# Both gates' projections moved out of the input projection into a stage of seven half-size products

## The chip, the cores and the metric

The kernel runs on one core of one Trainium2 chip. The metric is the device time of one execution in microseconds. Matrix products run on TensorE (PE in the profile), the other arithmetic on VectorE (DVE), ScalarE (ACT) and GpSimd (POOL). SyncE (SP) issues nearly all transfers.

## What is computed

A decoder layer with two parallel groups of heads over 1024 tokens of width 2048. One projection gives the inputs of both groups and their gates z_a and z_g:

```python
h = jnp.einsum('bsd,de->bse', x, w_in[l])
q_a, k_a, v_a, z_a, q_g, k_g, v_g, z_g, gk_lr = jnp.split(h, pts, axis=-1)
...
y_a = _swa_sink_attention(q_a', k_a', v_a', attn_sinks[l]) * jax.nn.silu(z_a)
...
y_g = (o_g.astype(x.dtype) * jax.nn.silu(z_g.reshape(B, S, GLA_HEADS, GLA_DV))).reshape(B, S, GLA_WIDTH)
y = jnp.einsum('bse,ed->bsd', jnp.concatenate([y_a, y_g], axis=-1), w_out[l])
x = _layer_norm(DN_ALPHA * x + y, ln_g[l], ln_b[l])
```

(The primes stand for the rotary positions.) Attention has 16 query heads of 64, 2 key heads, a window of 128 and a sink for each head. The second group is gated linear attention (GLA): 4 heads with keys of 128 and values of 256, a data-dependent decay, and an RMS norm on each head's output. z_a and z_g have 1024 columns each: together 2048 of the 5392 columns of w_in.

## The kernel before

Every fp32 product is three matmuls. `split` (L108) turns a tile into a rounded part, cast on ACT, and the rest, a subtraction on DVE; high x high, high x low and low x high are summed in PSUM.

The **input stage** runs the tokens in two halves H of 512. `half_jobs` (L491) makes a list of jobs from ORDER (L42), and each job projects x to 128 output features (K, V: the attention keys and values; a: a query tile of two heads; z: the attention gate of a tile; q, k: GLA; g, h: the two halves of a GLA head's gate) or, for v, to 256. `main_f` (L165) does a job in 48 matmuls of 128x512 into one of the three banks of the pool mm; `main_v` does a v job in 192 of 128x256. Behind each job its `evac` takes the bank over, and its `later` functions are put off by so many jobs (`run_later`, L648): attention of a query tile comes one job behind its projection, the stages of a GLA head (`gla_near`, `gla_far`, two `gla_pairs`) nought to three jobs behind v. A gate job's evac makes SiLU with tanh (`silu2`), multiplies it with the mixer's output (`attention_out`, `gla_out`) and stores the gated result to DRAM (`store_y`, buffer yd).

The mixers have one buffer of nearly everything. One attention head goes: ps (scores on PE), s (ACT copies, DVE puts in the masked part), nm (row maximum, DVE), four exponentials (ACT), s times the reciprocal sum (POOL, L278), pt (four transposes on PE), pm (DVE masks the transposed tile), po (the product with the values on PE). A GLA head begins with gk, the decays' product (`decays`), goes through seven levels of operands w and products pa, the transposes pk and the state products pg and pkv, and ends in the transposes po of `gla_out`. All of ps, pt, gk, pa, pk, pkv and the GLA po share the three banks of the pool sd; so has two.

`weight_sums` (L627), one for every second job, makes with four GpSimd subtractions the sums of blocks of w_out that the output stage needs, 32 in all, and stores them to DRAM (td). They and the projection weights come through the four raw buffers.

The **output stage** does y x w_out with seven products of half size in place of eight (Strassen in Winograd's form). `seq` (L818) has their order. Each runs over two column halves fp, eight k and four tiles t, 3 matmuls each (`product`, L739), into eight banks: the three of mm and five of op, which take the place of so and sd. `y_part` loads and adds blocks of y (POOL, L721), `w_part` loads eight weight tiles (pool wsp) for a half, and `collect` adds each product to its outputs. The layer norm runs behind the last ones.

The engines' orders are set when the program is built: a planner orders the instructions by its own estimates and by priority, which is the place in the program, raised by `high_priority` for loads and splits. On the chip each engine keeps that order and waits where something isn't ready.

Of the kernel before, what the change touches and what calls it, by code (L numbers as in the profile page):

```python
# [31 lines left out]
E_QA, E_KA, E_VA, E_ZA, E_QG, E_KG, E_ZG = 0, 8, 9, 10, 18, 22, 26  # L32
# [9 lines left out]
ORDER = [  # L42
    "K V q0 k0 v0 a0 z0 a1 z1 g0 h0 a2 z2 q1 k1 v1 a3 z3 g1 h1 a4 z4 q2 k2 v2 a5 z5 g2 h2 a6 z6 q3 k3 v3 a7 z7 g3 h3",
    "K V q0 k0 v0 a0 z0 a1 z1 g0 h0 a2 z2 q1 k1 v1 a3 z3 g1 h1 a4 z4 q2 k2 v2 a5 z5 g2 h2 a6 z6 q3 k3 v3 a7 z7 g3 h3",
]
# [30 lines left out]
def build(ctx: ExitStack, tc, xT, xr, w_e, w_v, w_gk, w_up, b_gk, cos_d, sin_d, cst_d, sinks, wn_d, w_out, g_d, b_d, out):  # L76
# [83 lines left out]
    td = [dr_p.tile([P, 16, 4, 256], F32, name=f"td{f}") for f in range(2)]  # L160
    ys_d = dr_p.tile([P, 8 * T], F32, name="ysum")
# [28 lines left out]

    def silu2(acc, pool, tag, bufs):

        t = pool.tile([P, T], F32, name=tag, tag=tag, bufs=bufs)
        A.activation(t, acc, AF.Tanh, scale=0.5)
        V.scalar_tensor_tensor(t, t, 1.0, acc, ALU.add, ALU.mult)
        return t
# [101 lines left out]
    def store_y(y, H, f):  # L298
        SP.dma_start(yd[H][f // 4][:, (f % 4) * T:(f % 4 + 1) * T], y)
# [166 lines left out]
    def gla_out(hd, gen, sz, H):  # L466
        for pr, on in gen:
            pt = sd.tile([P, 2, 2, P], F32, name="po", tag="sd")
            for u in range(2):
                for i in range(2):  # L470
                    PE.transpose(pt[:, u, i], on[:, i, u * P:u * P + P], ident)
            for u in range(2):
                c = slice(2 * pr * P, 2 * pr * P + 2 * P)
                z = sz[u][:, c].rearrange("p (i q) -> p i q", i=2)
# [16 lines left out]
    def half_jobs(H):  # L491
        c = ctxs[H]

        def qa(t):
# [5 lines left out]
            e_job(H, E_QA + t, evac, (None, later))  # L500

        def za(t):
            e_job(H, E_ZA + t, lambda acc: attention_out(t, c.pop(("po", t)), acc, H))
# [14 lines left out]
        def v_job(hd):  # L518
# [17 lines left out]
            jobs.append(Job([w_v[hd][:, :2048], w_v[hd][:, 2048:]], H, "v", evac, (near, far, pair, pair)))  # L536

        def zg(hd, u):
            def evac(acc):
                c["sz", hd, u] = silu2(acc, gp, f"szg{u}", 1)  # L540

            def later():
                gla_out(hd, c["on", hd], [c["sz", hd, 0], c["sz", hd, 1]], H)
            e_job(H, E_ZG + 2 * hd + u, evac, (None, later) if u else ())
# [7 lines left out]
        make = {"K": ka, "V": va, "q": q_job, "k": k_job, "v": v_job, "g": lambda hd: zg(hd, 0), "h": lambda hd: zg(hd, 1), "a": qa, "z": za}  # L552
        for j in ORDER[H].split():
            make[j[0]](*map(int, j[1:]))
# [72 lines left out]
    def weight_sums(n):  # L627

        f, k, u = n // 16, n % 16 // 2, n % 2
# [3 lines left out]
        for t, (eg, q) in ((b11, (f, 0)), (b12, (2 + f, 0)), (b21, (f, 2)), (b22, (2 + f, 2))):  # L633
            SP.dma_start(t, w_out[eg, q + k // 4][:, c])
# [4 lines left out]
        SP.dma_start(td[f][:, n % 16], r)  # L639
# [14 lines left out]
    i = 0  # L654
    while i < n:
# [43 lines left out]
    G.memset(eps, LN_EPS)  # L699

    def y_raw(h, g, k, tag):

        r = x_p.tile([P, T], F32, name="yr", tag=tag)
        with tc.high_priority(2000):
            SP.dma_start(r, yd[h][2 * g + k // 4][:, (k % 4) * T:(k % 4 + 1) * T])
        return r

    def y_part(i, k):

        at = {1: "00", 2: "01", 3: "01", 4: "11", 5: "10", 6: "10", 7: "00"}[i]  # L710
        a = y_raw(int(at[0]), int(at[1]), k, "xh")
        kept = ys_d[:, k * T:k * T + T]
        if i == 3:
            b = x_p.tile([P, T], F32, name="yr", tag="xl")
            with tc.high_priority(2000):
                SP.dma_start(b, kept)
            G.tensor_tensor(a, a, b, ALU.subtract)
        more = {5: ((1, 1, 1),), 6: ((1, 1, 1), (0, 0, -1)), 7: ((1, 0, -1),)}
        for n, (h, g, sign) in enumerate(more.get(i, ())):
            b = y_raw(h, g, k, "xl" if n % 2 == 0 else "xh")  # L720
# [5 lines left out]
    def w_part(i, fp, q, pool, tag):  # L726

        r = raw_p.tile([P, 2, 512], F32, name="raw", tag="raw")
        with tc.high_priority(2000):
            if i in (1, 2, 3):  # L730
                eg, w = {1: (fp, 0), 2: (fp, 2), 3: (2 + fp, 2)}[i]
                src = w_out[eg, w + q // 2][:, (q % 2) * 1024:(q % 2) * 1024 + 1024]
                SP.dma_start(r, src.rearrange("p (u c) -> p u c", u=2))
            else:
                j = {5: 0, 7: 1, 4: 2, 6: 3}[i]
                SP.dma_start(r.rearrange("p u (h c) -> p (u h) c", h=2), td[fp][:, 4 * q:4 * q + 4, j])
        return [split(r[:, u], pool, tag) for u in range(2)]

    def product(acc, y, w, t, k, first, last):  # L739
        (yh, yl), (wh, wl) = y, w  # L740
        c = slice(t * P, t * P + P)
        PE.matmul(acc, yh[:, c], wh, start=(first and k == 0), stop=False, skip_group_check=True)  # L742
# [169 lines left out]
```

## Time and profile before

| | us |
|---|---|
| median of 3 runs | 1437.87 (1437.31 to 1441.54) |
| the profiled execution | 1435.88 |
| its span, first to last instruction | 1433.7 |
| TensorE busy | 1414.9 (99%) |
| VectorE busy | 856.7 (60%) |
| ScalarE busy | 600.3 (42%) |
| GpSimd busy | 290.3 (20%) |

The input stage takes the first 1111 us, the output stage the rest. Matmul durations overlap in the trace, since PE is pipelined: what a matmul costs is read from the distance of the starts. A row of the timeline names the engine, the line, and out<-in by the program's names.

### The profile page before, as it was taken

What the parts mean: (1) busy time and instruction counts of PE and PEld (TensorE: products, weight loads), DVE (VectorE), ACT (ScalarE), POOL (GpSimd) and SP (SyncE); (2) the same over time, 40 slices, a digit from 0 to 9 for tenths busy, and PEclk for the clock granted to TensorE, in tenths of its full rate; (3) what the DMA queues carried; (4) which work ended last, traced back from release to release, by engine and by line L of the source; (5) the groups of instructions that cost most, each with busy time, mean ns of one, the idle gap of its engine ahead of it and who ended that gap; (6) DMA issues with size and microseconds to landing.
All of it is one profiled execution on the core that took longest, in us unless ns stands there. A gap on an engine that the chain in (4) does not pass through costs nothing.

```text
span 1433.7 us, 23435 instructions
## 1 busy us (share of the span) xinstructions
PE 1414.9 (99%) x8992; PEld 1181.0 (82%) x8992; DVE 856.7 (60%) x1481; ACT 600.3 (42%) x1279; POOL 290.3 (20%) x325
## 2 busy tenths in 40 slices
PE   8999999999999999999999999999999999999996
PEld 5888889888888976898888888988898888888885
DVE  5565556555655566565655555564566645466798
ACT  5544435435443445344435443443545324433320
POOL 0032212221311122213212221131101412122000
PEclk9999999999999999999999999999999999999998
DMA  8243344443434435543443334433325797665552
GB/s 318 86 148 128 111 147 131 135 133 107 144 131 134 133 127 175 168 157 113 159 133 123 115 131 136 138 112 118 104 95 163 239 362 230 216 218 189 172 208 117
DMA packets 99231, 222.36 MB, mean 155 GB/s; under 512 B 10800, under 2 KB 43568, under 8 KB 97968
## 3 DMA queue, kind: packets, MB, share of 16 engines
q1 hardware_dynamic: 97968, 218.78, 46.1%
q10 hardware_dynamic: 1152, 2.10, 0.4%
q8 instruction: 70, 1.15, 0.3%
q14 instruction: 41, 0.34, 0.1%
HBM read 180.47 MB, written 35.65 MB: 151 GB/s over the span
## 4 chain that ended last, share of the span: by engine, by line
PE 98%; DVE 1%; DMA 1%; ACT 0%; POOL 0%; SPq 0%; issue 0%; DVEq 0%; POOLq 0%
PE acc L172 18%; PE acc L174 18%; PE acc L173 17%; PE acco L742 7%; PE acco L743 7%; PE acco L744 7%; PE accv L186 4%; PE accv L188 4%; PE accv L187 4%; PE po L291 2%; PE pa L360 1%; PE ps L259 1%; PE ps L260 1%; PE pt L281 1%; PE lracc L310 1%; PE pg L405 1%
## 5 line engine op out<-in xcount | busy, mean ns | idle before, releaser
L113 DVE TENSOR_TENSOR wl<-raw,wh 128x512 fp32r<-128x512 f32 x440 | 331.6, 759 | 280.7 <-ACT wh L112 258.1
L112 ACT CAST wh<-raw 128x512 fp32r<-128x512 f32 x440 | 269.8, 620 | 416.9 <-PE acc L173 283.5
L172 PE MATMUL acc<-xh,wh 128*128 128x512 f32 x1088 | 429.4, 396 | 6.5 <-ACT wh L112 6.5
L174 PE MATMUL acc<-xh,wl 128*128 128x512 f32 x1088 | 427.1, 393 | 0.0
L173 PE MATMUL acc<-xl,wh 128*128 128x512 f32 x1088 | 426.9, 393 | 0.0
L172 PEld LDWEIGHTS acc<-xh,wh 128*128 128x128 f32 x1088 | 205.0, 188 | 53.8 <-ACT wh L112 8.4
L174 PEld LDWEIGHTS acc<-xh,wl 128*128 128x128 f32 x1088 | 204.8, 188 | 44.8 <-issue 1.4
L173 PEld LDWEIGHTS acc<-xl,wh 128*128 128x128 f32 x1088 | 205.0, 188 | 42.6 <-issue 2.2
L743 PE MATMUL acco<-wl,xh 128*128 128x512 f32 x416 | 161.9, 389 | 0.0
L742 PE MATMUL acco<-wh,xh 128*128 128x512 f32 x416 | 160.7, 390 | 0.2
L744 PE MATMUL acco<-wh,xl 128*128 128x512 f32 x416 | 160.8, 389 | 0.0
L186 PE MATMUL accv<-wh,xh 128*128 128x256 f32 x512 | 145.3, 284 | 0.0
L188 PE MATMUL accv<-wh,xl 128*128 128x256 f32 x512 | 145.0, 283 | 0.0
L187 PE MATMUL accv<-wl,xh 128*128 128x256 f32 x512 | 144.8, 283 | 0.0
L186 PEld LDWEIGHTS accv<-wh,xh 128*128 128x128 f32 x512 | 98.1, 192 | 1.2 <-issue 0.7
L188 PEld LDWEIGHTS accv<-wh,xl 128*128 128x128 f32 x512 | 98.1, 192 | 0.6 <-issue 0.3
L187 PEld LDWEIGHTS accv<-wl,xh 128*128 128x128 f32 x512 | 98.2, 192 | 0.5
L742 PEld LDWEIGHTS acco<-wh,xh 128*128 128x128 f32 x416 | 78.1, 188 | 17.3 <-ACT xh L112 1.3
L744 PEld LDWEIGHTS acco<-wh,xl 128*128 128x128 f32 x416 | 78.1, 188 | 16.7 <-DVE xl L113 0.4
L743 PEld LDWEIGHTS acco<-wl,xh 128*128 128x128 f32 x416 | 78.1, 188 | 15.8
L113 DVE TENSOR_TENSOR xl<-yr,xh 128x512 fp32r<-128x512 f32 x56 | 38.5, 687 | 77.4 <-ACT xh L112 76.9
L112 ACT CAST xh<-yr 128x512 fp32r<-128x512 f32 x56 | 34.6, 620 | 118.4 <-POOL yr L721 66.9
(169 smaller groups left out, 1686.7 us busy)
## 6 DMA issues: line engine op xcount, KB each, us to landing
raw<-in_w_e_dram SPq DMA_DIRECT2D x134, 512.0 KB, 3.9
yr<-yd SPq DMA_DIRECT2D x88, 256.0 KB, 4.8
raw<-in_w_v_dram SPq DMA_DIRECT2D x32, 512.0 KB, 4.2
raw<-in_w_out_dram SPq DMA_DIRECT2D x128, 128.0 KB, 2.7
td<-raw SPq DMA_DIRECT2D x32, 512.0 KB, 3.5
raw<-td SPq DMA_DIRECT2D x32, 512.0 KB, 4.6
raw<-in_w_out_dram SPq DMA_DIRECT2D x24, 512.0 KB, 4.0
raw<-in_xT_dram SPq DMA_DIRECT2D x15, 512.0 KB, 4.7
```

Of the source, the lines that this page charges most:

```text
L112: A.copy(hi, src)
L113: V.tensor_tensor(lo, src, hi.bitcast(F32), ALU.subtract)
L172: PE.matmul(acc, wh[:, c], xh, start=(k == 0), stop=False)
L173: PE.matmul(acc, wh[:, c], xl, start=False, stop=False)
L174: PE.matmul(acc, wl[:, c], xh, start=False, stop=(k == KT - 1))
L186: PE.matmul(o, xh[:, t], wh[:, c], start=(k == 0 and tb % 2 == 0), stop=False, skip_group_check=True)
L187: PE.matmul(o, xh[:, t], wl[:, c], start=False, stop=False, skip_group_check=True)
L188: PE.matmul(o, xl[:, t], wh[:, c], start=False, stop=(k == KT - 1), skip_group_check=True)
L291: x = PE.matmul(po[64 * u:64 * u + 64, a:b], vt[:, j + 1, 64 * g:64 * g + 64], pms[u][:, a2:b2], start=(len(heads) < 2), stop=(j == NB - 1 ...
L742: PE.matmul(acc, yh[:, c], wh, start=(first and k == 0), stop=False, skip_group_check=True)
L743: PE.matmul(acc, yh[:, c], wl, start=False, stop=False, skip_group_check=True)
L744: PE.matmul(acc, yl[:, c], wh, start=False, stop=(last and k == 7), skip_group_check=True)
```

## The change

The gate jobs z, g and h are gone from ORDER: a half has 22 jobs in place of 38. The mixers scale their outputs on ScalarE and store them ungated (buffer od), as `later` functions of the a and v jobs. A new stage between input and output stage makes z = x w_z by the same seven products of half size that the output stage uses, with the weight as the stationary side. `collect_gates` adds the products up; where a block of z is complete, `gate` loads the stored mixer result, makes SiLU, multiplies and stores the gated result where the output stage reads it. The block sums of w_z are 32 more weight sums, so 64 are spread over 44 jobs.

```diff
-E_QA, E_KA, E_VA, E_ZA, E_QG, E_KG, E_ZG = 0, 8, 9, 10, 18, 22, 26
+E_QA, E_KA, E_VA, E_QG, E_KG = 0, 8, 9, 10, 14
...
-ORDER = [
-    "K V q0 k0 v0 a0 z0 a1 z1 g0 h0 a2 z2 q1 k1 v1 a3 z3 g1 h1 a4 z4 q2 k2 v2 a5 z5 g2 h2 a6 z6 q3 k3 v3 a7 z7 g3 h3",
...
+ORDER = "K V q0 k0 v0 a0 q1 k1 v1 a1 a2 q2 k2 v2 a3 a4 q3 k3 v3 a5 a6 a7"
...
-    def attention_out(t, po, acc, H):
-        sz = silu2(acc, ap, "sza", 1)
-        V.scalar_tensor_tensor(sz, po, 0.5, sz, ALU.mult, ALU.mult)
-        store_y(sz, H, t)
+    def attention_out(t, po, H):
+        o = ap.tile([P, T], F32, name="oa", tag="oa", bufs=1)
+        A.mul(o, po, 0.5)
+        store(o, od, H, t)
...
-    def gla_out(hd, gen, sz, H):
+    def gla_out(hd, gen, H):
+        og = [gp.tile([P, T], F32, name=f"og{u}", tag=f"og{u}", bufs=1) for u in range(2)]
...
-                V.scalar_tensor_tensor(z, pt[:, u], wnh[:, u:u + 1], z, ALU.mult, ALU.mult)
+                A.activation(o, pt[:, u], AF.Copy, scale=wnh[:, u:u + 1])
...
-            store_y(sz[u], H, 8 + 2 * hd + u)
+            store(og[u], od, H, 8 + 2 * hd + u)
...
-            e_job(H, E_QA + t, evac, (None, later))
+            e_job(H, E_QA + t, evac, (None, later, out))
...
-            jobs.append(Job([w_v[hd][:, :2048], w_v[hd][:, 2048:]], H, "v", evac, (near, far, pair, pair)))
+            jobs.append(Job([w_v[hd][:, :2048], w_v[hd][:, 2048:]], H, "v", evac, (near, far, pair, pair, out)))
...
+        w, tw, n = (w_z, td[0], n) if n < 32 else (w_out, td[1], n - 32)
...
-        if i > 5 and i % 2 == 0 and i // 2 - 3 < 32:
-            weight_sums(i // 2 - 3)
         i += len(group)
+        while summed < 64 * (i - 4) / (n - 4):
+            weight_sums(summed)
+            summed += 1
...
+            return xT[h, q][:, c] if s == 0 else yd[h][q][:, c]
...
+        (lh, ll), (rh, rl) = (y, w) if s else (w, y)
...
+    def gate(z, H, f):
+
+        o, sz = roll(0), roll(1)
+        SP.dma_start(o, od[H][f // 4][:, (f % 4) * T:(f % 4 + 1) * T])
+        A.activation(sz, z, AF.Tanh, scale=0.5)
+        V.scalar_tensor_tensor(sz, sz, 1.0, z, ALU.add, ALU.mult)
+        V.tensor_tensor(o, o, sz, ALU.mult)
+        store(o, yd, H, f)
+
+    def collect_gates(i, fp, t, acc):
+        u1, u2, u3 = (part(n, fp, t) for n in (0, 2, 1))
+        f = 4 * fp + t
+        if i in (1, 6, 7):
+            A.copy({1: u1, 6: u2, 7: u3}[i], acc)
+        elif i == 4:
+            gate(acc, 1, f)
+        elif i == 2:
+            V.tensor_tensor(u1, u1, acc, ALU.add)
+            gate(u1, 0, f)
+        elif i == 5:
+            V.tensor_tensor(u3, u3, acc, ALU.add)
+            gate(u3, 1, 8 + f)
+        else:
+            V.tensor_tensor(u2, u2, acc, ALU.add)
+            gate(u2, 0, 8 + f)
...
-    FIRST, LAST = (1, 5), (4, 3)
+    FIRST, LAST = (1, 5, 2), (4, 3, 2)
...
-    seq = (1, 6, 7, 4, 5, 3, 2)
+    seq = [(0, i) for i in (1, 6, 7, 4, 2, 5, 3)] + [(1, i) for i in (1, 6, 7, 4, 5, 3, 2)]
```

The names in the orders below are the matmuls' output and inputs: acc and accv are projections, acco the products of the half-size stages, gk the first matmuls of a GLA head, po of L283 or L291 the end of an attention tile, po of L464 or L471 a GLA head's output transposes.

TensorE at the last gk of the program (GLA head 3 of the second half), before:

```order
L187 MATMUL accv<-wl,xh 128x256
L281 MATMUL pt<-cst,s 128x128 x4
L327 MATMUL gk<-lr,wuph 128x512
L328 MATMUL gk<-lr,wupl 128x512
L188 MATMUL accv<-wh,xl 128x256
L186 MATMUL accv<-wh,xh 128x256
```

And after:

```order
L173 MATMUL acc<-xh,wl 128x512
L319 MATMUL gk<-lr,wuph 128x512
L283 MATMUL po<-pm,vt 64x128
L283 MATMUL po<-pm,vt 64x256 x6
L283 MATMUL po<-pm,vt 64x128 x2
L320 MATMUL gk<-lr,wupl 128x512
L352 MATMUL pa<-kq 32x32 x16
L171 MATMUL acc<-xh,wh 128x512
L172 MATMUL acc<-xl,wh 128x512
```

Before, projections worth 282 matmuls of 128x512 stand behind this gk; after, six.

TensorE at the last po of an attention tile, before:

```order
L742 MATMUL acco<-wh,xh 128x512
L743 MATMUL acco<-wl,xh 128x512
L291 MATMUL po<-pm,vt 64x128
L291 MATMUL po<-pm,vt 64x256 x6
L291 MATMUL po<-pm,vt 64x128 x2
L405 MATMUL pg<-sph,qdh 128x256
L406 MATMUL pg<-spl,qdh 128x256
L407 MATMUL pg<-sph,qdl 128x256
L744 MATMUL acco<-wh,xl 128x512
```

And after:

```order
L251 MATMUL ps<-kh_96,qs_9333 128x256
L252 MATMUL ps<-kl_98,qs_9333 128x256
L283 MATMUL po<-pm,vt 64x128
L273 MATMUL pt<-cst,s 128x128 x4
L464 MATMUL po<-cst,on 128x128 x8
L283 MATMUL po<-pm,vt 64x128
L283 MATMUL po<-pm,vt 64x256 x6
L283 MATMUL po<-pm,vt 64x128 x2
L736 MATMUL acco<-xh,wh 128x512
L737 MATMUL acco<-xl,wh 128x512
```

Before, 41 products acco stand ahead of this po and 31 between it and the last GLA transposes, and the mixers' matmuls lie singly among them. After, 72 acco stand ahead of it, all of them before the second head of tile a5, and behind those come the last heads' ps, pt and po with no acco between.

## Rows read from the trace of the kernel before

**Rows 1.** The page: busy us (share) xinstructions; the chain that ended last.
```profile
PE 1414.9 (99%) x8992; PEld 1181.0 (82%) x8992; DVE 856.7 (60%) x1481; ACT 600.3 (42%) x1279; POOL 290.3 (20%) x325
...
PE 98%; DVE 1%; DMA 1%; ACT 0%; POOL 0%; SPq 0%; issue 0%; DVEq 0%; POOLq 0%
```

**Rows 2.** Timeline of PE, input stage: start, us, engine, line, operation, out<-in.
```profile
1062.17 0.39 PE L174 MATMUL acc<-xh,wl 128*128 128x512 f32 x1
...
1070.34 0.39 PE L174 MATMUL acc<-xh,wl 128*128 128x512 f32 x1
```

**Rows 3.** Windows, us: PE, PEld, DVE, ACT, POOL busy (x), PEclk, DMA, GB/s.
```profile
300.00:540.00 240.00, 240.00 (x1730) 202.62 (x1729) 140.78 (x255) 105.48 (x227) 49.92 (x62) 1.00 0.41 133
...
1280.00:1340.00 60.00, 60.00 (x266) 49.71 (x265) 34.30 (x50) 17.16 (x31) 14.99 (x11) 1.00 0.64 203
1340.00:1400.00 60.00, 60.00 (x266) 49.70 (x265) 56.49 (x89) 20.44 (x38) 0.00 (x0) 1.00 0.51 177
```

**Rows 4.** Timeline of PE, DVE, ACT and POOL: one attention head's step.
```profile
890.55 0.60 PE L281 MATMUL pt<-cst,s 128*128 128x128 f32 x4
...
891.19 1.23 DVE L283 TENSOR_TENSOR pm<-pt,cst 128x1024 f32<-128x1024 f32 x1 [1.99 <-PE pt L281]
...
891.72 0.80 ACT L262 COPY s<-ps 128x256 f32<-128x256 f32 x2 [0.53 <-PE ps L260]
...
897.66 1.04 POOL L278 TENSOR_TENSOR s<-s,sm 128x512 f32<-128x512 f32 x1 [7.05 <-DVE sm L277]
...
902.04 0.60 PE L281 MATMUL pt<-cst,s 128*128 128x128 f32 x4
```

**Rows 5.** Timeline of PE and POOL: the same step of another tile.
```profile
839.41 0.60 PE L281 MATMUL pt<-cst,s 128*128 128x128 f32 x4
...
846.84 1.04 POOL L278 TENSOR_TENSOR s<-s,sm 128x512 f32<-128x512 f32 x1 [10.97 <-DVE sm L277]
```

**Rows 6.** Timeline of PE, DVE and ACT: a GLA head from gk to kd.
```profile
902.40 0.48 PE L327 MATMUL gk<-lr,wuph 128*128 128x512 f32 x1
...
918.40 1.23 DVE L343 TENSOR_TENSOR dd<-dd 128x512 f32<-128x512 f32 x1
...
927.92 0.63 ACT L341 ACTIVATE w<-dd 128x512 f32<-128x512 f32 x1
...
936.01 1.23 DVE L388 TENSOR_TENSOR kq<-kq,dd 128x1024 f32<-128x1024 f32 x1 [0.27 <-ACT dd L387]
...
945.61 0.60 PE L392 MATMUL pk<-cst,kq 128*128 128x128 f32 x4
...
947.64 0.69 DVE L399 TENSOR_TENSOR kdl<-pk,kdh 128x512 fp32r<-128x512 f32 x1
```

**Rows 7.** The chain in order of time: start, us, what; the mixers' small matmuls.
```profile
796.10 1.36 PE pa L360 x99
...
906.46 1.88 PE po L291 x16
```

**Rows 8.** Windows at the end, columns as in rows 3; timeline of PE, start.
```profile
1420.00:1424.00 4.00, 1.56 (x7) 0.94 (x5) 3.90 (x5) 0.00 (x0) 0.00 (x0) 1.00 0.16 66
1424.00:1428.00 4.00, 0.00 (x0) 0.00 (x0) 3.86 (x8) 0.29 (x1) 0.00 (x0) 0.64 0.48 197
1428.00:1432.00 4.00, 0.00 (x0) 0.00 (x0) 1.89 (x3) 0.00 (x0) 0.00 (x0) 0.50 0.76 262
...
8.79 0.63 PE L172 MATMUL acc<-xh,wh 128*128 128x512 f32 x1
...
11.35 0.63 PE L174 MATMUL acc<-xh,wl 128*128 128x512 f32 x1
```

**Rows 9.** Lines of DVE: shapes xcount | busy us, mean ns | idle before.
```profile
L113 DVE TENSOR_TENSOR wl<-raw,wh 128x512 fp32r<-128x512 f32 x440 | 331.6, 759 | 280.7 <-ACT wh L112 258.1 <-PE acc L173 16.8 <-PE pt L281 2.0
...
L113 DVE TENSOR_TENSOR xl<-yr,xh 128x512 fp32r<-128x512 f32 x56 | 38.5, 687 | 77.4 <-ACT xh L112 76.9
...
L195 DVE SCALAR_TENSOR_TENSOR sza<-sza,acc 128x512 f32<-128x512 f32 x16 | 10.9, 680 | 0.0
```

More of the change, by code (lines that the diff above doesn't have):

```diff
@@ L652, in run_later @@
             f()
-    i = 0
+    i, summed = 0, 0
     while i < n:
@@ L699, in build, with y_part, raw, block @@
     G.memset(eps, LN_EPS)
[L701 to L712, printed above, removed]
-        if i == 3:
[L714 to L720, printed above, removed]
+    weight = [w_z, w_out]
+    def y_part(s, i, k):
+        def raw(src, tag):
+            r = x_p.tile([P, T], F32, name="yr", tag=tag)
+            with tc.high_priority(2000):
+                SP.dma_start(r, src)
+            return r
+        def block(h, g):
+            c = slice((k % 4) * T, (k % 4 + 1) * T)
+            q = 2 * g + k // 4
+            return xT[h, q][:, c] if s == 0 else yd[h][q][:, c]
+        kept = ys_d[s][:, k * T:k * T + T]
+        first, *more = {1: ((0, 0, 1),), 2: ((0, 1, 1),), 3: ((0, 1, 1),), 4: ((1, 1, 1),), 5: ((1, 0, 1), (1, 1, 1)),
+                        6: ((1, 0, 1), (1, 1, 1), (0, 0, -1)), 7: ((0, 0, 1), (1, 0, -1))}[i]
+        a = raw(block(*first[:2]), "xh")
+        if i == 3:
+            G.tensor_tensor(a, a, raw(kept, "xl"), ALU.subtract)
+        for n, (h, g, sign) in enumerate(more):
+            b = raw(block(h, g), "xl" if n % 2 == 0 else "xh")
             G.tensor_tensor(a, a, b, ALU.add if sign > 0 else ALU.subtract)
@@ L735, in w_part, with product, part, roll @@
                 j = {5: 0, 7: 1, 4: 2, 6: 3}[i]
-                SP.dma_start(r.rearrange("p u (h c) -> p (u h) c", h=2), td[fp][:, 4 * q:4 * q + 4, j])
+                SP.dma_start(r.rearrange("p u (h c) -> p (u h) c", h=2), td[s][fp][:, 4 * q:4 * q + 4, j])
         return [split(r[:, u], pool, tag) for u in range(2)]
-    def product(acc, y, w, t, k, first, last):
-        (yh, yl), (wh, wl) = y, w
+    def product(acc, s, y, w, t, k, first, last):
+        (lh, ll), (rh, rl) = (y, w) if s else (w, y)
         c = slice(t * P, t * P + P)
-        PE.matmul(acc, yh[:, c], wh, start=(first and k == 0), stop=False, skip_group_check=True)
-        PE.matmul(acc, yh[:, c], wl, start=False, stop=False, skip_group_check=True)
-        PE.matmul(acc, yl[:, c], wh, start=False, stop=(last and k == 7), skip_group_check=True)
+        PE.matmul(acc, lh[:, c], rh, start=(first and k == 0), stop=False, skip_group_check=True)
+        PE.matmul(acc, lh[:, c], rl, start=False, stop=False, skip_group_check=True)
+        PE.matmul(acc, ll[:, c], rh, start=False, stop=(last and k == 7), skip_group_check=True)
+    def part(n, fp, t):
+        return pre[2 * n + fp][:, t * T:t * T + T]
+    rolls = [0, 0]
+    def roll(n):
+        rolls[n] += 1
+        return pre[6 + n][:, rolls[n] % 4 * T:rolls[n] % 4 * T + T]
+    def gate(z, H, f):
[21 more added lines that the diff above has]
+            gate(u2, 0, 8 + f)
     def norm(tb, tail):
@@ L816, in banks @@
         return out
-    seq = (1, 6, 7, 4, 5, 3, 2)
-    ys = {(seq[0], k): y_part(seq[0], k) for k in range(2)}
-    for n, i in enumerate(seq[:-1]):
-        if i in (1, 4):
+    seq = [(0, i) for i in (1, 6, 7, 4, 2, 5, 3)] + [(1, i) for i in (1, 6, 7, 4, 5, 3, 2)]
+    ys = {(*seq[0], k): y_part(*seq[0], k) for k in range(2)}
+    for n, (s, i) in enumerate(seq[:-1]):
+        if s and i in (1, 4):
             for t in range(NB):
```

83 lines of the change are left out of this document (39 added, 44 removed).

## The prediction

> **What bounds the kernel now.** I read the page's busy shares and its chain of waits first: TensorE is busy 99% of the span, and the chain that ended last is PE for 98% [rows 1]. So what is taken off TensorE shortens the run, as long as something keeps TensorE fed. Next the price of a product. In the input stage 36 of them, two of whose rows are shown, run from 1062.17 to 1070.34 us: 0.2270 us each [rows 2]. In the output stage 266 fill 60 us: 0.2256 each [rows 3]. Third, what runs beside: in 300 to 540 us VectorE is busy 141 of 240 us and GpSimd 50, while PE has no gap [rows 3]. Last, the two chains of the mixers that hide behind the products: the step of one attention head [rows 4, 5] and the recurrence of one GLA head [rows 6].
>
> **The change, part by part.** *Products.* 32 gate jobs of 48 matmuls go: 1536 x 0.2270 = 348.7 us. Seven products of 2 column halves x 8 k x 4 tiles x 3 come: 1344 x 0.2256 = 303.2 us. Net **-45.5 us**, all on the engine that sets the end.
>
> *The gate stage itself.* It has the form of the output stage, which runs without a gap on PE even in 1340 to 1400 us, where VectorE is busy 56.5 of 60 [rows 3]. Its heaviest products (the fifth to the seventh) ask VectorE for 16 weight splits at 0.759, 8 input splits at 0.687 and 8 x 3 steps of 0.68 (an add, the SiLU, the gate) [rows 9]: 12.1 + 5.5 + 16.3 = 34 us, against 192 x 0.2256 = 43.3 us of PE. Price 0, hidden by PE's own 43.3; where VectorE took more, each microsecond over that would cost one. The stored mixer results come back as 32 loads of 256 KB on SP, four of them ahead of use, beside weight loads that are the output stage's own. Price 0 as well: a half product, 21 us, lies over each four.
>
> *Weight sums.* 32 more sets of four GpSimd subtractions, 8 of them a mixer head. GpSimd was a fifth busy [rows 3] and stays under half. But each set holds one of the four raw buffers through which the weights come, and stands in GpSimd's order ahead of the softmax scaling that the head step needs. What that costs PE no row shows. Bounds: 0 (GpSimd now sits idle behind such sets with no gap on PE) and one head step of 8 us for half of the 8 GLA heads, 30 us. I take 5, near the row that shows no gap.
>
> *The cover.* This decides. The mixers' work on the small engines is the same, but 22 jobs a half lie over it instead of 38, and the gate jobs were the last of all. In the order of before, the last recurrence starts (gk) some 280 products ahead of the last projection, and the drain is over while the output stage's first 72 products run. In the order of after, the last gk stands 6 matmuls ahead of the end of the projections. Behind it come 72 gate products, all that three free banks and eight weight buffers allow, then only the mixers' own small matmuls, and the next gate product stands behind the last po. Between that gk and that gate product TensorE must wait for a chain that it feeds itself:
> - The last recurrence. From gk (902.40) to the last near operand (919.63) 17.2 us; the far operands and the decays, 927.92 to 937.24, 9.3; from the transposes (945.61) to the end of kd's split (948.33) 2.7 [rows 6]. Sum 29.2 us.
> - Six head steps, of tiles a5, a6 and a7. In the order of after each head's scores stand behind the transposes of the head before, so the steps don't overlap. One step, from the start of pt to the end of the next head's scaled s: 890.55 to 898.70 and 839.41 to 847.88, 8.15 and 8.5 us [rows 4, 5]. I take 8.2. The next pt then stood 3.3 us behind that end, in queue behind products, so the spacing was 11.5; behind no products that goes. The first step shares VectorE with the recurrence's states: 11. Sum 11 + 5 x 8.2 = 52.
> - The last mask 1.23 [rows 4], then the eight output transposes and nine po, some 2 [rows 7]. Sum 3.
>
> That is 84 us. TensorE's own work in it: 78 products, 17.6 us, and the small ones: some 120 pa at 1.36 / 99 = 0.014 us, 1.7, and some 156 scores, transposes, po and state products, taken at the 1.88 / 16 = 0.118 of a po [rows 7], 18.3: 20 us. So 84 - 38 = 46 us stay empty. Idle, TensorE can also lose its clock: after its last matmul at the end of before the granted clock reads 0.64 and then 0.50 of full speed, the lower of its two levels, 1.2 GHz [rows 8]. On the path that doubles some 0.9 us a step, 5 us in all, and the first products behind the drain: the program's first stand 0.427 apart (8.79 to 11.35 us, six of them [rows 8]) instead of 0.227, so a dozen cost 2.5. **+53.5 us.** Bounds: a step at 7 (the rows' own durations, nothing queued between) with the clock kept gives +40; at the spacing of 11.5 us, where the gate stage's loads and sums get in the way, +71.
>
> What the rows show here (the products lie over the mixers without a gap, [rows 2, 3]) has a rule beside it. The Trainium skill, "Perfetto Trace Analysis", Optimization Strategy, says of a kernel with several regimes that interleaving them can improve it; this change does the reverse, and takes a regime of pure products out of one of mixed work. By that rule the saving is not whole, and the sum is above 1392; by the rows alone it is the sum below.
>
> *Sum*, against the profiled execution's own span: 1433.7 - 45.5 + 53.5 + 5 = 1446.7 us. The execution took 1435.88, 2.2 over its span, and the median of the runs is 1437.87, 2.0 over that: forecast **1451 us** (+0.9%).
>
> **The rivals.** *The drain is short.* If two heads' steps ran side by side, the drain would be three steps shorter: 84 - 25 = 59 us, 21 of them empty: 1437.9 - 45.5 + 21 + 5 = 1418 us. For it: VectorE and ScalarE are each busy for half a step. Against it: the order of TensorE is fixed, each ps behind the pt before. *The saving comes whole:* -45.5, 1392 us; the next gate products would have to hide all of the chain, and the banks don't let them. The Trainium skill, "Perfetto Trace Analysis", Identifying the Most-Contended Engine, tells one to optimise the engine of highest occupancy first, which here would give this time; the rows bear it out only where a cover is left.
>
> *The input stage itself becomes bound by the mixers* (far slower). Between two recurrences lie now six jobs' worth of products, 288 x 0.2270 = 65 us, and some 20 of small matmuls: 85 us. The chain between them is 29 + four steps + some 8 to the next gk: 70 us at 8.2 a step, 83 at 11.5. At 85 it begins to decide, and a GpSimd set or two on each step puts it there: with 6 to 8 us a head over 8 heads, +55, some 1505 us. For it: the order of after has its recurrences trailing the jobs by up to three. Against it: 15 us of slack by the rows.
>
> *Gain and loss cancel:* a drain of 40 to 45 empty us and no stall elsewhere, 1434 to 1442.
>
> **How the numbers follow.** A measurement of this kernel can tell about 0.3%, 4 us, from no change. Forecast (slower by 0.3% to 3%) 0.60; input stage bound, 1482 and more, 0.12; cancelled 0.12; short drain, 1400 to 1433, 0.13; whole saving 0.03. Slower 0.72, same 0.12, faster 0.16. The range leaves out the whole saving, half of the short drain and half of the far slower: 1422 to 1490. The bounds of the drain alone give 1437.9 - 45.5 + 40 = 1432 to 1463, and 0 to 30 for the sums come on top: 1493, of which the range keeps all but the last few.
>
> **What would show it.** PE's count of 128x512 matmuls falls by 192. The 40 slices of PE show full up to some 740 us, then two or three slices near half, with PEclk below 9 in one or more, then full to the end. In that stretch TensorE waits for the scaled s of GpSimd (pt) and the masks of VectorE (po), six steps 8 to 10 us apart. The gate stage's seven products take 43 us each. I am wrong about the drain if that stretch lasts under 70 us; about the stage if gaps stand ahead of 700 us; about the gate stage if PE has gaps behind 840.

## The result, and the profile after

The changed kernel takes 1562.62 us (median of 3 runs, 1559.86 to 1565.59) against 1437.87: 1.086 times as long, 95% interval 1.082 to 1.090. The forecast was 1451, the range 1422 to 1490. The sign was right; the size was not. The profiled execution has a span of 1563.8 us, 117 more than the sum of 1446.7.

The page of the changed kernel: span, busy times (the last number counts instructions), then TensorE, GpSimd and the granted clock in 40 slices of 39 us, and the chain that ended last by engine.

```profile
span 1563.8 us, 24084 instructions
PE 1423.1 (91%) x8800; PEld 1181.5 (76%) x8800; DVE 934.7 (60%) x1529; ACT 645.6 (41%) x1391; POOL 464.9 (30%) x493
PE   8989989999978989898998649999999999999996
POOL 0433345543454244443433510200111133022000
PEclk9998989999989989899998679999999999999999
PE 44%; DMA 16%; DVE 10%; POOL 7%; issue 5%; ACT 3%; SPq 2%; POOLq 0%; DVEq 0%; ACTq 0%
```

The 192 matmuls are gone (8992 to 8800). But where [rows 1, 2] showed TensorE without a gap and 98% of the chain on it, eights now stand in the PE row from the third slice on, ahead of the dip that was forecast (6 and 4 in the slices from 860 us), and the chain is on TensorE for 44%; transfers, VectorE and GpSimd hold most of the rest.

Four rows date the stages of the changed kernel. Each is a group of TensorE's instructions: count, shortest/median/longest ns, first to last start.

```profile
L173 PE MATMUL acc<-xh,wl x576: 387/389/797, 8.7 to 840.4; 128*128 128x512 f32 x192
L319 PE MATMUL gk<-lr,wuph x8: 391/397/503, 59.5 to 836.2; 128*128 128x512 f32 x8
L283 PE MATMUL po<-pm,vt x288: 272/379/689, 142.7 to 942.2; 128*64 128x256 f32 x88, 128*64 128x128 f32 x56
L736 PE MATMUL acco<-wh,xh x416: 387/389/503, 1230.8 to 1545.4; 128*128 128x512 f32 x139
```

The last projection starts at 840.4 us, the last gk at 836.2, the last po at 942.2, the output stage at 1230.8. The same four dates of the other kernels below are read from the same rows of their traces:

| us | last projection | last gk | last po | output stage begins | span | us median |
|---|---|---|---|---|---|---|
| before | 1110.2 | 1033.2 | 1123.8 | 1111.1 | 1433.7 | 1437.9 |
| changed | 840.4 | 836.2 | 942.2 | 1230.8 | 1563.8 | 1562.6 |
| no sums | 756.2 | 761.4 | 865.3 | 1153.9 | 1487.8 | 1488.2 |
| before, 64 sums | 1120.5 | 1043.5 | 1134.2 | 1121.5 | 1445.7 | 1447.9 |
| rope's queue | 823.2 | 828.4 | 932.2 | 1220.8 | 1549.9 | 1552.8 |
| sums late | 793.5 | 798.4 | 905.9 | 1223.3 | 1548.7 | 1544.2 |
| no arithmetic | 785.3 | 790.5 | 895.4 | 1184.1 | 1515.8 | 1518.1 |
| arithmetic only | 796.7 | 801.8 | 905.8 | 1194.5 | 1520.3 | 1523.5 |
| few bytes | 768.7 | 774.0 | 876.0 | 1164.7 | 1493.0 | 1490.6 |
| write only | 818.9 | 823.1 | 926.9 | 1215.6 | 1540.7 | 1542.3 |
| stores on GpSimd | 838.5 | 840.9 | 941.9 | 1232.3 | 1562.9 | 1565.9 |
| sums on VectorE | 853.5 | 863.5 | 963.6 | 1256.3 | 1589.4 | 1584.6 |
| short drain | 758.5 | 763.6 | 822.5 | 1126.4 | 1455.4 | 1459.2 |
| head 3 early | 837.3 | 737.0 | 934.1 | 1224.2 | 1552.4 | 1555.6 |

(The planner makes the order anew for each kernel, so a few microseconds between two of them can be the order's. The first column is the last of a product's three matmuls; expectations below that say 784.8 for the run without arithmetic speak of the first of the three.)

With these dates the 117 us divide. The forecast's input stage ends at 1110.2 - 348.7 = 761.5 us, and 20 us of the mixers' own matmuls move from it into the drain: the last gk stands at some 741. It came at 836.2, **95 late** where 5 was allowed. From the last gk to the last po lie **106.0 us**, where 84 and 5 for the clock were forecast: 17 more. From there to the output stage 288.6 us, where 1272 products at 0.2256 and the cold start give 289.5: right. The output stage takes 333.0, before it took 322.6: **10 more**. 90 + 17 - 1 + 10 = 116.

So the larger part of the miss is in the input stage, which I had held to be hidden. Two stretches of the changed kernel, then a part of the second (length, busy us of TensorE with its matmuls, weight loads, VectorE, ScalarE, GpSimd, granted clock, DMA share, GB/s):

```profile
200.00:340.00 140.00, 131.68 (x956) 112.70 (x957) 92.10 (x162) 65.52 (x163) 66.17 (x73) 0.95 0.53 173
340.00:480.00 140.00, 127.17 (x869) 100.68 (x869) 92.66 (x163) 67.25 (x160) 59.86 (x67) 0.96 0.62 201
440.00:460.00 20.00, 14.82 (x59) 12.26 (x60) 12.51 (x24) 6.97 (x22) 13.05 (x13) 0.75 0.65 206
```

In [rows 3] the same stage had no gap. Here TensorE stands for 8 and 13 us of 140, and the clock isn't whole. One gap, at 112 us, by the changed kernel's timeline (the brackets tell how long the engine stood before the instruction, and for whom):

```profile
111.18 0.58 ACT L390 CAST kdh<-pk 128x512 fp32r<-128x512 f32 x1
116.49 0.69 DVE L199 TENSOR_TENSOR rq<-rq,cos 128x512 f32<-128x512 f32 x1 [4.61 <-DMA rs<-rq]
117.22 0.69 DVE L391 TENSOR_TENSOR kdl<-pk,kdh 128x512 fp32r<-128x512 f32 x1
117.96 0.58 PE L399 MATMUL pkv<-vg,kdl 128*128 128x256 f32 x1 [5.64 <-DVE kdl L391]
```

kdh is done at 111.76, so kdl could start; but a rope step (rq) stands ahead of it in VectorE's order and waits for a transfer. TensorE, with the state product pkv next in its own order, stands for 5.6 us, and the projections queued behind pkv stand with it.

### The profile page after: what moved, and what is told of

Its sections match the earlier page's. It is cut to its first block, busy times and chain, and to the rows that moved or that the text cites. A ratio compares the mean times of both kernels' runs of the same rounds, so it can differ in the third digit from the quotient of the medians.

```text
span 1563.8 us, 24084 instructions
## 1 busy us (share of the span) xinstructions
PE 1423.1 (91%) x8800; PEld 1181.5 (76%) x8800; DVE 934.7 (60%) x1529; ACT 645.6 (41%) x1391; POOL 464.9 (30%) x493
## 4 chain that ended last, share of the span: by engine, by line
PE 44%; DMA 16%; DVE 10%; POOL 7%; issue 5%; ACT 3%; SPq 2%; POOLq 0%; DVEq 0%; ACTq 0%
PE acco L737 9%; PE acco L738 9%; PE acco L736 9%; DMA yr<-yd 5%; DMA raw<-in_w_out_dram 4%; PE acc L172 2%; DVE wl L110 2%; PE acc L173 2%; PE acc L171 2%; PE accv L187 2%; PE accv L186 2%; PE accv L185 2%; DMA td<-raw 2%; DMA rs<-rq 2%; POOL yr L714 1%
## 5 line engine op out<-in xcount | busy, mean ns | idle before, releaser
L171 PE MATMUL acc<-xh,wh 128*128 128x512 f32 x576 | 232.9, 406 | 8.8 <-ACT wh L109 6.9
L172 PE MATMUL acc<-xl,wh 128*128 128x512 f32 x576 | 233.6, 406 | 0.0
L173 PE MATMUL acc<-xh,wl 128*128 128x512 f32 x576 | 232.8, 404 | 0.0
L714 POOL TENSOR_TENSOR yr<-yr 128x512 f32<-128x512 f32 x64 | 88.7, 1387 | 378.0 <-DMA yr<-yd 172.7
L736 PE MATMUL acco<-xh,wh 128*128 128x512 f32 x448 | 176.3, 393 | 2.9 <-ACT rq L194 2.9
L737 PE MATMUL acco<-xl,wh 128*128 128x512 f32 x448 | 175.8, 392 | 0.0
L738 PE MATMUL acco<-xh,wl 128*128 128x512 f32 x448 | 175.8, 393 | 0.0
L171 PEld LDWEIGHTS acc<-xh,wh 128*128 128x128 f32 x576 | 112.8, 196 | 35.2 <-ACT wh L109 7.9
L173 PEld LDWEIGHTS acc<-xh,wl 128*128 128x128 f32 x576 | 112.7, 196 | 26.0 <-issue 1.6
L172 PEld LDWEIGHTS acc<-xl,wh 128*128 128x128 f32 x576 | 112.7, 196 | 25.8 <-issue 1.8
```

Source lines behind the costliest of these rows:

```text
L171: PE.matmul(acc, wh[:, c], xh, start=(k == 0), stop=False)
L172: PE.matmul(acc, wh[:, c], xl, start=False, stop=False)
L173: PE.matmul(acc, wl[:, c], xh, start=False, stop=(k == KT - 1))
L714: G.tensor_tensor(a, a, b, ALU.add if sign > 0 else ALU.subtract)
L736: PE.matmul(acc, lh[:, c], rh, start=(first and k == 0), stop=False, skip_group_check=True)
L737: PE.matmul(acc, lh[:, c], rl, start=False, stop=False, skip_group_check=True)
```

## Experiments

Theory S: the weight sums, 64 in 840 us where 32 stood in 1111, hold up the mixers' chain. The rival, theory C: 22 jobs a half are too thin a cover whatever the sums do.

**The sums left out.** The loop that calls `weight_sums` goes, and `w_part` reads a plain block.

```diff
-        while summed < 64 * (i - 4) / (n - 4):
-            weight_sums(summed)
-            summed += 1
```

> The changed kernel without any of its 64 weight sums: the products that use a sum take a plain block of the weight of the same size instead, so loads and products of the two last stages keep their number, and only the sums' loads, GpSimd subtractions and stores in the input stage are left out. Theory S (the sums, three times as dense as before, hold up the rope's transfers, the weight loads and GpSimd's softmax scaling): the time falls to what was forecast without them, 1445 to 1470 us, and TensorE's windows of 50 us ahead of 850 us are full. Theory C (22 jobs a half are too thin a cover for the mixers' own chains, sums or not): it stays at 1530 us or more, and the gaps ahead of 850 us stay.

Measured: 1488.2 us, ratio 1.036 (1.033 to 1.038), 74 us less than the changed kernel. The same two stretches of this run, and the dates of its last projection and its last gk:

```profile
200.00:340.00 140.00, 138.70 (x1071) 120.95 (x1070) 84.66 (x167) 68.84 (x174) 21.55 (x23) 1.00 0.28 89
340.00:480.00 140.00, 134.96 (x957) 108.32 (x955) 93.76 (x170) 73.30 (x173) 23.10 (x22) 1.00 0.38 118
L173 PE MATMUL acc<-xh,wl x576: 387/389/632, 8.4 to 756.2; 128*128 128x512 f32 x192
L319 PE MATMUL gk<-lr,wuph x8: 391/398/502, 59.9 to 761.4; 128*128 128x512 f32 x8
```

TensorE is nearly full and its clock whole in both stretches. The last gk, from which the drain runs, comes 75 us earlier (761.4, not 836.2), about what the spans differ by (76.0). The last projection moves by 84, but 9 of these are the order's: it stands 4 us behind the last gk in the changed kernel and 5 ahead of it here. So the gk is what counts below, also where an expectation speaks of the 84. The run missed the expected 1445 to 1470 because the last gk still comes 20 us behind 741, and because the drain (103.9 us) and the output stage (333.9) kept their length. So theory S holds for the input stage, and nearly all that the sums cost lies there. The thinner cover by itself costs at most the 20 us: TensorE stands for 13 us of this run between 60 and 740 us, and 3 are gate products that its order puts ahead of the gk.

**The sums under the old cover.** The kernel before, 64 sums.

```diff
-        if i > 5 and i % 2 == 0 and i // 2 - 3 < 32:
-            weight_sums(i // 2 - 3)
+        while summed < 64 * (i - 4) / (n - 4):
+            weight_sums(summed)
+            summed += 1
```

> The kernel before, with 64 weight sums in place of 32 (each set of blocks summed twice, the second into a buffer that nobody reads), about one behind each job. Theory S: the sums cost by themselves, 20 to 60 us over the kernel before, 1460 to 1500 us. Theory C: under the full cover of 38 jobs a half the added sums are hidden, 1435 to 1445 us.

Measured: 1447.9 us, ratio 1.0075 (1.005 to 1.010): 11 us over the runs of the kernel before that were taken with it, 10 of them in the input stage (last gk 1033.2 to 1043.5). Neither expectation: 32 more sums aren't free under 38 jobs a half, but they cost little more than a quarter of the 37 or 38 us that 32 cost under 22 (the run with half of the sums late, below). Sums and cover count together, then. The slack behind that can be read from the end of one query tile's last transposes (pt) to the scores of the next tile's first head (ps) and its pt. First the kernel before, then the changed one:

```profile
428.25 0.60 PE L281 MATMUL pt<-cst,s 128*128 128x128 f32 x4
455.75 0.22 PE L259 MATMUL ps<-kh,qs 128*128 128x128 f32 x1
466.69 0.60 PE L281 MATMUL pt<-cst,s 128*128 128x128 f32 x4
```

```profile
338.63 0.66 PE L273 MATMUL pt<-cst,s 128*128 128x128 f32 x4 [1.83 <-POOL s L270]
345.28 0.22 PE L251 MATMUL ps<-kh,qs 128*128 128x128 f32 x1
```

Before, 27 us lie between two tiles of this chain, and what comes late can be made up there. After the change 6.7 us are left, and the pt ahead of them already makes TensorE wait for GpSimd's scaled s. (Of the places ahead of the drain where no gk stands between two tiles, six of eight have 21 to 27 us before, the others 8 and 1; all six have 7 or less after.) The run without the sums has 6.7 us here too (305.55 to 312.27), so the distance is the cover's doing. That it is the slack which the sums overran is a reading; no run varied it by itself. Each of the seven distances between the eight gk is longer in the changed kernel than without the sums, by 2 to 18 us (95.8 and 82.1, 116.3 and 101.0, 102.1 and 97.7, 158.0 and 139.9, 70.7 and 63.6, 127.0 and 112.7, 106.8 and 104.5), together the 75 us: the loss is everywhere, not one stall.

**Which part of a sum costs.** Four kernels take it apart. In the first two the transfers or the arithmetic are missing:

```diff
-        G.tensor_tensor(b11, b12, b11, ALU.subtract)
-        G.tensor_tensor(b12, b22, b12, ALU.subtract)
-        G.tensor_tensor(b22, b22, b11, ALU.subtract)
-        G.tensor_tensor(b21, b21, b22, ALU.subtract)
```

> The changed kernel whose 64 weight sums keep their loads, their raw buffers and their stores, but not the four GpSimd subtractions between them (the blocks are stored as they were loaded). Without the sums at all the input stage ended 84 us earlier (last projection at 756.2 instead of 840.4 us). If what costs is GpSimd's arithmetic, standing in its order ahead of the softmax scaling and the recurrence's steps, most of the 84 us come back here: last projection at 755 to 775 us, 1485 to 1505 us in all. If it is the transfers (SP's queue, the raw buffers, the memory's bandwidth), it stays: last projection at 815 us or later, 1540 us or more.

> The opposite half: the 64 sums' loads, raw buffers and stores are left out, and GpSimd's work stays, as five subtractions of 128x192 on resident constants in place of four of 128x256 (the products that use a sum take a plain block of the same size). If GpSimd's order is the cause: last projection at 815 us or later, 1540 us or more. If the transfers are: 755 to 775 us, 1485 to 1505 us. If the cost needs both (GpSimd waiting in order for late loads), both this and the run without arithmetic come out near 1490 to 1510 us.

Measured: 1518.1 us without the arithmetic, 1523.5 with it alone, both between their expectations; the last gk at 790.5 and 801.8. Neither is the cause by itself: the transfers cost 29 us over no sums (790.5 - 761.4), the arithmetic 40 (801.8 - 761.4), together 69 of the 75. The second, whose diff isn't shown (five subtractions on resident constants in place of a set), needs care: with no load to wait for, the planner put most of the 320 subtractions into the first 300 us, nine tenths of GpSimd from 100 us on.

Then each half was split again: the transfers at an eighth of their bytes, and the arithmetic as writes that read nothing.

```diff
-            SP.dma_start(t, w[eg, q + k // 4][:, c])
+            SP.dma_start(t[:, :32], w[eg, q + k // 4][:, c][:, :32])
...
-        SP.dma_start(tw[f][:, n % 16], r)
+        SP.dma_start(tw[f][:, n % 16, :, :32], r[:, :, :32])
```

> The changed kernel without the subtractions, as in the run without arithmetic (1518.1 us, last projection at 784.8 us), and each of the sums' loads and stores cut to an eighth of its bytes (the products that use a sum take a plain block of the same size). The number of transfers, their place in SP's order and the raw buffers stay. If the bytes cost (64 MB in 840 us more on the DMA engines), the last projection ends at 755 to 765 us and the time is 1486 to 1496. If the queue and the buffers cost, it stays at 778 us or later, 1510 us or more.

```diff
-        G.tensor_tensor(b11, b12, b11, ALU.subtract)
...
+        for _ in range(3):
+            G.memset(r, 0.0)
+        G.memset(b11, 0.0)
```

> The changed kernel with its sums' loads, raw buffers and stores, where GpSimd fills the buffer three times and a quarter with zeros (some 3.4 us, as long as the four subtractions) in place of the subtractions: it occupies GpSimd's order as before, but reads no operand from SBUF. The last projection ended at 840.4 us with the subtractions and at 784.8 without any arithmetic. If GpSimd's occupied order is what costs the 55 us, it ends at 820 us or later here (1540 us or more). If the cost is that subtractions of GpSimd and two-operand instructions of VectorE hold each other up (VectorE's decay sum takes 857 ns on average with the sums, 753 without), it ends at 780 to 805 us (1510 to 1530 us), and VectorE's means are those of the run without sums.

Measured: 1490.6 and 1542.3 us. The first is in the range for the bytes, its last projection (768.7 us) 4 us past it; the second is in that of the occupied order, its last projection (818.9) 1 us short of it. A set's writes take 3 x 0.954 + 0.313 = 3.2 us of GpSimd, its subtractions 3.4. With the runs above this makes a staircase of the last gk: no sums 761, the transfers' number and buffers 774 (+13), their bytes 790 (+16), GpSimd's order occupied and the buffers held meanwhile 823 (+33), subtractions in place of writes 836 (+13). In the medians the same steps are 2, 28, 24 and 20, since the later stages differ between the kernels too; so a step is known to some 12 us only. In this order of taking apart no step is more than 33 of the 75: none is the cause by itself.

What the last step does is seen in VectorE's own rows: its decay sum (dd, two operands in SBUF), its mask (pm, one operand in PSUM) and GpSimd's part, up to 750 us (count, then busy us, mean ns, idle before). The changed kernel, no sums, write only, in that order:

```profile
L335 DVE TENSOR_TENSOR dd<-dd 128x512 f32<-128x512 f32 x46 | 39.4, 856 | 0.0
L275 DVE TENSOR_TENSOR pm<-pt,cst 128x1024 f32<-128x1024 f32 x22 | 26.9, 1222 | 19.8 <-PE pt L273 19.7
```

```profile
L335 DVE TENSOR_TENSOR dd<-dd 128x512 f32<-128x512 f32 x49 | 36.9, 753 | 0.0
L275 DVE TENSOR_TENSOR pm<-pt,cst 128x1024 f32<-128x1024 f32 x25 | 30.6, 1222 | 18.5 <-PE pt L273 18.3
```

```profile
L335 DVE TENSOR_TENSOR dd<-dd 128x512 f32<-128x512 f32 x49 | 36.7, 750 | 0.0
L275 DVE TENSOR_TENSOR pm<-pt,cst 128x1024 f32<-128x1024 f32 x22 | 26.9, 1224 | 28.5 <-PE pt L273 28.5
L625 POOL MEMSET raw<- 128x1024 f32 x180 | 170.9, 954 | 250.9 <-DMA raw<-in_w_out_dram 104.4 <-DMA raw<-in_w_z_dram 96.0 <-DVE w L334 21.2
```

dd takes 856 ns on average with GpSimd's subtractions (most take 0.68 us, the longest 1.76), 753 without them and 750 with GpSimd's writes; pm stays at 1222 to 1224. The Trainium skill, "SBUF — State Buffer", Who interferes with whom, says that a VectorE instruction with two SBUF inputs contends with a GpSimd instruction that reads SBUF, not with one that only writes it; these rows agree. The step also holds the 0.2 us a set by which the subtractions are longer than the writes; the two weren't separated.

**Repairs.** Four changes to where the work stands and waits, all with the full computation. First the rope's transfers on ScalarE's queue:

```diff
-            SP.dma_start(sw[32 * a:32 * a + 32], q[32 * b:32 * b + 32])
+            A.dma_start(sw[32 * a:32 * a + 32], q[32 * b:32 * b + 32])
```

> The changed kernel, the four swap transfers of each rope issued on ScalarE's queue instead of SP's. If these transfers come late because they stand in SP's order behind the stores of the sums (VectorE then stands in order behind them), the time falls by 25 to 60 us, to 1500 to 1540 us, and VectorE's wait for rs at the rope falls from 8.7 us at most to some 3. If the queue isn't the cause it stays within 8 us of 1562.

Measured: 1552.8 us, ratio 1.081 (1.078 to 1.083); the last gk comes 8 us earlier and the whole takes 10 us less, little more than the 8 of "the queue isn't the cause" and far from the 25 of the other. VectorE's waits for rs up to 840 us (in total, times, longest), the changed kernel first:

```profile
DVE rq L199 <- DMA rs<-rq: 52.6, 11, 8.7
```

```profile
DVE rq L199 <- DMA rs<-rq: 27.8, 12, 4.3
```

The gap at 112 us was of this kind; what this repair gives back of such gaps is a tenth of the input stage's 75 us. Next the sums' stores on GpSimd's queue:

```diff
-        SP.dma_start(tw[f][:, n % 16], r)
+        G.dma_start(tw[f][:, n % 16], r)
```

> The changed kernel, the sums' stores issued on GpSimd's queue, behind the subtractions that they wait for, instead of on SP's, where each holds up every load and rope transfer issued behind it until GpSimd is done (236.6 us of waiting in 59 stores). If that blocked queue is the cause: last projection at 775 to 800 us, 1500 to 1525 us. If not: within 8 us of 1562, or slower where GpSimd's issuing costs it time.

Measured: 1565.9 us, ratio 1.092 (1.089 to 1.094): no gain. SP's waits in question, the changed kernel and this one:

```profile
SPq L628 <- POOL raw L627: 236.6, 59, 8.0
```

```profile
SPq L100 <- DMA td<-raw: 193.9, 36, 9.6
SPq L623 <- DMA td<-raw: 76.2, 18, 7.4
```

SP no longer waits for GpSimd ahead of the store. It waits instead, at the next weight load, for the store to land, since that load needs the raw buffer. So the blocked queue alone was not the limit. These waits point to the buffer behind it; a kernel with more raw buffers wasn't run. Next half of the sums in the gate stage:

```diff
-        while summed < 64 * (i - 4) / (n - 4):
+        while summed < 32 * (i - 4) / (n - 4):
...
+                if s == 0 and summed < 64 and (8 * fp + k) % 3 == 0:
+                    weight_sums(summed)
+                    summed += 1
```

> The changed kernel with the 32 sums of the output weight moved out of the input stage into the gate stage, six beside each of its products; the input stage keeps the 32 of the gate weight. The density in the input stage is then half. Theory S: half or more of the some 100 us lost there comes back, 1490 to 1515 us, at little cost in the gate stage, whose GpSimd is a quarter busy or less. Theory C: 1550 to 1565 us.

Measured: 1544.2 us, ratio 1.074 (1.072 to 1.076), neither expectation. The input stage gives back 38 us (last gk 836.2 to 798.4), so the cost there is linear: 37 us for the first 32 sums, 38 for the next. But from the last po to the output stage it now takes 317.4 us in place of 288.6: 32 sums cost 29 there, so the gate stage hides a sum hardly better. The likely reason is that its transfers are dense already, 0.73 of the DMA engines without sums (950 to 1230 us of the changed kernel), and 0.91 with them (960 to 1223 us of this one; DMA row, from the 25th slice on):

```profile
PE   8999999998899898998983689999889999899996
DMA  8544434335543333444484269888999797776452
```

The fourth moved the four subtractions to VectorE:

```diff
-        G.tensor_tensor(b11, b12, b11, ALU.subtract)
+        V.tensor_tensor(b11, b12, b11, ALU.subtract)
```

> The changed kernel with the sums' four subtractions on VectorE in place of GpSimd: 256 of them, some 0.4 us each by the halves of its 512-wide rows, 100 us more on an engine that was busy 430 of the input stage's 840 us. If GpSimd's part of the cost (its order, or its holding up of VectorE) is larger than 100 us spread over VectorE's gaps, the time falls, 1525 to 1545 us; if VectorE's own order is the tighter one, it rises to 1570 us or more.

Measured: 1584.6 us, ratio 1.102 (1.097 to 1.106), slower by 22 than the changed kernel. A subtraction takes 0.445 us there in place of 0.857, and still costs more. I put that down to VectorE standing in each step of both mixers, GpSimd in a few; no run shows it by itself.

**The drain.** Without sums, the attention of the second half's last two tiles left out:

```diff
-                c["po", t] = attention(t, c.pop(("acc", t)), c["tabs"], H)
+                acc = c.pop(("acc", t))
+                c["po", t] = acc if H == 1 and t > 5 else attention(t, acc, c["tabs"], H)
```

> The changed kernel without its weight sums, as in the run without sums (1488.2 us), and with the attention of the last two tiles of the second half left out (the projected tile is stored in place of the attention's result). That takes four of the six head steps out of the drain between the last gk and the last po, which took 104 us in that run. If the drain is a serial chain of head steps, as forecast, it falls by four steps of 8.2 to 11 us: 1444 to 1456 us. If the steps lie beside the recurrence, or loads of the gate stage set its end, it falls by less than 20: over 1468 us.

Measured: 1459.2 us, 29 under the run without sums, between the two expectations. The drain itself fell by 45 us (103.9 to 58.9), four steps at 11.3: serial, as forecast. 15 came back behind it (303.9 us to the output stage in place of 288.6): the two stored tiles hold two of the three free banks, so only 24 gate products in place of 72 stand ahead of the last po in TensorE's order (48 x 0.2256 = 11 us), and the first one behind it waited 3.2 us.

The drain's steps in the changed kernel: the last gk, then the six pt, in TensorE's rows.

```profile
836.17 0.40 PE L319 MATMUL gk<-lr,wuph 128*128 128x512 f32 x1
885.55 1.11 PE L273 MATMUL pt<-cst,s 128*128 128x128 f32 x4
899.80 0.60 PE L273 MATMUL pt<-cst,s 128*128 128x128 f32 x4
911.21 1.11 PE L273 MATMUL pt<-cst,s 128*128 128x128 f32 x4 [6.19 <-POOL s L270]
920.16 1.12 PE L273 MATMUL pt<-cst,s 128*128 128x128 f32 x4 [5.56 <-POOL s L270]
928.39 1.11 PE L273 MATMUL pt<-cst,s 128*128 128x128 f32 x4 [2.70 <-POOL s L270]
936.62 1.12 PE L273 MATMUL pt<-cst,s 128*128 128x128 f32 x4 [4.90 <-POOL eps L690]
```

The steps are 14.3, 11.4, 9.0, 8.2, 8.2. The last two have the forecast's 8.2 to the digit. The first two share the engines with the recurrence's states, and the first with 24 of the 72 gate products: the pt at 899.80 came without a wait of TensorE's, since products stood ahead of it. GpSimd gets in the way of the drain too, where it adds blocks of x for the gate stage (yr). One such row of GpSimd, then two of VectorE:

```profile
848.09 3.50 POOL L714 TENSOR_TENSOR yr<-yr 128x512 f32<-128x512 f32 x2
850.40 2.14 DVE L335 TENSOR_TENSOR dd<-dd 128x512 f32<-128x512 f32 x1
854.78 0.68 DVE L335 TENSOR_TENSOR dd<-dd 128x512 f32<-128x512 f32 x1
```

dd takes 2.14 us beside two such adds and 0.68 where GpSimd is idle. And the scaled s of the step that took 14.3 us starts at 896.79, 2.4 us after its sm was done, right behind another yr.

Last, an ORDER that takes the recurrence out of the drain:

```diff
-ORDER = "K V q0 k0 v0 a0 q1 k1 v1 a1 a2 q2 k2 v2 a3 a4 q3 k3 v3 a5 a6 a7"
+ORDER = "K V q0 k0 v0 a0 q1 k1 v1 a1 q2 k2 v2 a2 q3 k3 v3 a3 a4 a5 a6 a7"
```

> The changed kernel with another ORDER: the GLA heads of a half stand one query tile apart, and four query tiles without a head stand behind the last. In TensorE's order the last gk then comes 295 products ahead of the last projection (6 in the changed kernel), and 8 head steps stand behind that projection instead of a recurrence and 6 steps. By the forecast's own prices (8.2 us a step) the drain from the last projection to the last po falls from 102 us to 62 to 70 and the time to 1520 to 1535 us, if the input stage stays at 840. If the recurrences, closer together, then bind the input stage, what the drain gives is lost there: 1550 us or more.

Measured: 1555.6 us, ratio 1.083 (1.081 to 1.085), 7 less than the changed kernel. The input stage didn't suffer, but the drain from the last projection (837.3) to the last po (934.1) is 97 us, not 62 to 70; the time is in the range that was named for recurrences that bind the input stage, but for another reason. Three neighbouring steps of it:

```profile
857.95 0.60 PE L273 MATMUL pt<-cst,s 128*128 128x128 f32 x4
874.86 1.11 PE L273 MATMUL pt<-cst,s 128*128 128x128 f32 x4 [6.64 <-POOL s L270]
886.22 0.60 PE L273 MATMUL pt<-cst,s 128*128 128x128 f32 x4
```

16.9 and 11.4; all seven are 11.4, 16.9, 11.4, 17.0, 9.8, 8.2 and 7.1. Between the first two, TensorE's order has the po of one tile (862.54 to 866.1) ahead of the scores of the next, and its masks stood on VectorE behind the next tile's rope. A step of 8.2 is the price of a head whose rope is long done and whose scores stand right behind the pt ahead, not of every head.

No form of the changed kernel with the full computation came within 7% of the kernel before, and even without any sums the change costs 3.6%.

## Why the prediction was wrong, point by point

TensorE's longest wait of the changed kernel's output stage, from 1231 us on (us in total, times, longest), for the second point:

```profile
PE acco L737 <- DVE wl L110: 8.8, 13, 2.7
```

- *Products.* Right: 8800 matmuls, and the gate stage runs at the forecast's pace once the last po is through (288.6 us against 289.5).
- *The gate stage itself.* Price 0 was right inside it; TensorE has no gap from 950 to 1230 us. But as I read the order, its last sums and SiLUs stand on VectorE ahead of the output stage's weight splits: TensorE waits 8.8 us in 13 places there for wl, the longest 2.7, where [rows 3] had no gap. The output stage takes 325 to 334 us over all the kernels with a gate stage, 322.6 and 324.2 in the two without; which of it is VectorE's load and which the planner's order stays open.
- *Weight sums: the step that failed.* I took 5 us, "near the row that shows no gap", of bounds 0 and 30; it was 75 (74 between the medians with and without sums). The row [rows 3] was of a stretch with some 27 us between two tiles of the chain, where a price stays hidden; I used it for a stretch with 7. The upper bound was too low as well: a head step at half of the heads is near what GpSimd's occupied order cost (33 by the staircase), and leaves out the transfers (29) and the last step, with the holding up of VectorE (13). And for the up to 20 us that the thinner cover costs the input stage without any sums, the forecast's sum had nothing; only the rival below did.
- *The drain.* Serial, as forecast, and 106 us for 84 and 5. From gk to the end of kd's split (876.1) 39.9 us, not 29.2; then 9.5 and 51.1 to the last pt, where 52 was taken for all six steps; 5.6 to the last po, not 3. The term that was mis-sized is the price of the recurrence and of the first steps, taken from [rows 4 to 6], the best of their kind; of the 45.9 us that [rows 6] lasted, 29.2 were counted. In the drain the pa wait 0.5 to 3.9 us each for VectorE's w, and gate products lie between. And GpSimd's adds of x (yr, above) lengthen VectorE's steps, as only the upper bound had it. What each of the three took isn't settled.
- *The rivals.* "The input stage itself becomes bound by the mixers" is what happened. Its account, a GpSimd set or two on each step filling 15 us of slack, is near the runs; its 6 to 8 us a head was 75 / 8 = 9.4 for the sums, and 95 / 8 = 12 with what the thinner cover costs. Its time, some 1505, was still 58 us short. It had 0.12 because I held the 15 us against it without charging the eight sums a head (27 us of GpSimd) to the same chain. The short drain didn't come.
- *What would show it.* "About the stage if gaps stand ahead of 700 us": they stand from the third slice on, and that was the right place to look.

## What to carry to other kernels

A step that is free beside a full engine is free by that engine's cover; where a change thins the cover, charge everything that was free under it anew, against the slack that is left, and not from rows of the old place. Look for that slack in the trace first: here 27 us between two tiles of the hidden chain before, 7 after. And price a serial chain that is laid bare by more than one row of each step: the best rows gave 84 us here, 89 with the clock, the trace 106.

## What the runs showed of the hardware that I had not expected

- Gaps cost twice. The same 8800 matmuls are busy 1423.1 us in the changed kernel and 1396.6 without the sums: 26 of the 76 us between their spans are matmuls that ran slower, at a granted clock of 0.94 to 0.96 in the stretches of the input stage from 60 us on (0.75 in 440 to 460 us, 14.82 of 20 us busy) against 0.96 to 1.00. In the changed kernel TensorE waits 2.07 us ahead of the pt at 828.35; the granted clock from 829 to 832 us is 0.51, the level of 1.2 GHz, and the products from 830.75 to 832.03 start 0.43 us apart. From 833 on it is 1.00, 2.4 GHz, and they start 0.23 apart. So this stall among products cost the products behind it half of their clock.
- GpSimd's subtractions lengthen VectorE's dd, with two operands in SBUF, by 14% on average (753 to 856 ns) at a GpSimd share of some four tenths, and leave pm, with one operand in PSUM, alone (1222 ns); writes of nearly the same length don't lengthen dd either (750). In the staircase the step from writes to subtractions is 13 us, 20 in the medians.
